# A trunk kernel on one core: pooling as doubled sums on DVE, eight buffers in the second norm, output weights scaled without GpSimd

## The chip, the cores and the metric

The kernel runs on one core of a Trainium2 chip. The metric is the device time of one execution in microseconds (us); a version is measured in several runs and judged by their median. The engines are called by their short names: PE multiplies matrices (PEld is its loading of weights), DVE is the vector engine, ACT the scalar engine, POOL is GpSimd, and SP issues transfers.

## The reference

What is computed is a decoder trunk of two layers over 1024 tokens of width 1024, in float32. Each layer has a mixer and a mixture of experts, both behind an RMS norm that is modulated by a conditioning vector:

```python
mod = (jax.nn.silu(c) @ w_mod[i] + b_mod[i])[:, None, :]
shift1, scale1, gate1, shift2, scale2, gate2 = jnp.split(mod, 6, axis=-1)
h = rmsnorm(x, norm_gain[i, 0]) * (1.0 + scale1) + shift1
y = pool_mixer(...) if i == 0 else gla_mixer(...)
x = x + gate1 * y
h = rmsnorm(x, norm_gain[i, 1]) * (1.0 + scale2) + shift2
x = x + gate2 * hier_moe(h, ...)
```

The pooling mixer takes, for four groups of 256 channels, the mean over the last 2, 4, 8 or 16 tokens (fewer at the start of the sequence) minus the token itself, multiplies it by a block-diagonal matrix, adds a bias and scales. The GLA mixer of the second layer is a chunked gated linear attention that ends in an output product with `gla_w_out`. The mixture of experts sends each token to two of 64 experts.

## The kernel before

The stages follow one another on one core, and each reads what the one ahead of it wrote.

**First norm and pooling.** `X[t]` (t = 0 to 7) holds 128 tokens by 1024 channels. `rows_load` (L169) brings one slice of the modulation weights `w_mod` into a ring of six slots, `rows_use` (L181) multiplies it on PE, and `mods(lo, hi)` uses slices `lo` to `hi - 1` and starts the load of the slice six further on; there are 24 slices, and six loads of GLA input weights (L831) follow them in the ring. Slices 0 to 7 give the first norm's shift, scale and gate. `xn_tile` (L240, L236, L237, L242) squares on ACT, takes the root, inverts on DVE and scales the tile into `xh[t % 3]`. `mix(t)` pools on PE: a product with a band matrix per group (L847, `band` or `first`), and a second one with the tail of the tile ahead (L850, `prev`); the result is the transposed, pooled tile `dT[t]` (L852). The band matrices are built on DVE (L811 to L818).

**The pooling's output.** Once slices 0 to 7 are in, `pw` is scaled by columns and rows (L218, L225, L869), `Q1` is the bias row (L865), GpSimd adds it to every tile (L884), and `mix_out(t)` multiplies `dT[t]` by `pw` on PE (L878) and adds the result to `X[t]` on DVE (L881). Between the tiles stand slices 8 to 15, two for each pair of tiles.

**Second norm.** Tile by tile: `xn_tile` into `xnb[t % 2]`, `route_turn` (a store to `h_d`, L260, and eight transposes, L250, drained by ACT at L257 and DVE at L255), one slice of the modulation (16 to 23), and the router's product (L268, L269). The two buffers `xnb` are read by the store to `h_d`. `route` then sorts the tokens, and the first layer's experts begin; their weights come on SP's queue (L514, L515).

**Between the layers.** During the experts, pieces ("units") of the GLA input product run on PE (L1041) from a list that `run_units(n)` works off. After the last expert the eighth tile is normed and turned (`prep_norm`, `prep_out`), `scale_wo` works out a scale for the output weights in three steps (L1107, L1114, L225 with L1122), and all engines meet a branch for lists of over 128 tokens (L1178), whose body isn't run with these inputs. The order on PE here is the order in which the code is written.

**GLA.** Behind the branch the rest of the units, the gates of tiles 0 and 1 (`gl_gate`, L1247 to L1275) and `split_wo` (L1128: each of eight output weight blocks times the scale, four on DVE and four on GpSimd; L1129 and L1130: split into two float16 parts) come ahead of the scores (L1283 to L1288), the mixing (L1312 to L1334), the turning (L1342) and the output product (L1353), tile by tile.

Of the kernel before, what the change touches and what calls it, by code (L numbers as in the profile page):

```python
# [11 lines left out]
AF = mybir.ActivationFunctionType  # L12
# [5 lines left out]
NT = 8  # L18
# [18 lines left out]
def trunk_kernel(ctx, tc, x_in, c_in, norm_gain, w_mod, b_mod, pool_w, pool_b, pool_scale,  # L37
# [765 lines left out]
    V.memset(XGt, 0.0)  # L803
    V.memset(part(15, 7, 1024), 0.0)
    m01 = part(15, 6, 128)
    rw = part(15, 6.5, 128)
    band = [part(1, 8 + g, 128) for g in range(4)]
    prev = [part(1, 8.5 + g, 128) for g in range(4)]
    first = [part(15, 8 + 0.5 * g, 128) for g in range(4)]
    for g, w in enumerate(WINDOWS):  # L810
        V.tensor_scalar(m01, dm, 0.0, None, op0=OP.is_ge)  # L811
        V.scalar_tensor_tensor(m01, dm, float(w), m01, op0=OP.is_lt, op1=OP.mult)
        V.scalar_tensor_tensor(band[g], m01, 1.0 / w, ident, op0=OP.mult, op1=OP.subtract)
        V.tensor_scalar(rw, slot_no, 1.0, float(w), op0=OP.add, op1=OP.min)
        V.reciprocal(rw, rw)
        V.tensor_tensor(m01, m01, rw, op=OP.mult)
        V.tensor_tensor(first[g], m01, ident, op=OP.subtract)
        V.tensor_scalar(prev[g], dm, float(w - 128), 1.0 / w, op0=OP.is_lt, op1=OP.mult)  # L818
# [15 lines left out]
    pcol = part(15, 10, 16)  # L834
    xh = [part(8, 4 * i, 1024) for i in range(3)]
# [24 lines left out]
    mod_scale(0, 0)  # L860
    V.tensor_tensor(pcol[:, 0:8], sec(0, 2), C2[:, 16:24], op=OP.mult)
    V.tensor_tensor(pcol[:, 8:16], pcol[:, 0:8], C2[:, 8:16], op=OP.mult)
    for half in range(2):
        s = slice(half * 512, half * 512 + 512)
        S.copy(Q1[:, s], row_psum(pcol[:, 8:16], half, dg[0]))  # L865
        p = row_psum(pcol[:, 0:8], half, dg[1])
        for j in range(4):
            kc = 4 * half + j
            V.scalar_tensor_tensor(pw[:, kc, :], pw[:, kc, :], modA[:, 0, 0, kc:kc + 1],  # L869
                                   p[:, j // 2 * 256:j // 2 * 256 + 256], op0=OP.mult, op1=OP.mult)  # L870
# [12 lines left out]
    for t in range(NT):  # L883
        G.tensor_tensor(X[t], X[t], Q1, op=OP.add)  # L884
    for t in range(4):
        mods(8 + 2 * t, 10 + 2 * t)
        mix_out(2 * t)
        mix_out(2 * t + 1)
    mod_scale(0, 1)
    gate2_rows(0, dg)  # L890
    for t in range(NT):
        xn_tile(t, xnb[t % 2], xnb[t % 2], 1)
        route_turn(t, 0, xnb[t % 2], hTb[t % 2])
        mods(16 + t, 17 + t)
        route_logits(t, hTb[t % 2], wr, L, brow)
# [117 lines left out]
    def prep_out(j):  # L1013
        turn_tile(1, 0, xs, lambda kc: xsv[:, kc, :], gmul, gadd)
        for k in (slice(0, 4), slice(4, 8)):
# [138 lines left out]
    with tc.manual_schedule(engines={ET.PE}):  # L1154
# [7 lines left out]
        prep_norm(7)  # L1162
        run_units(len(units))
# [199 lines left out]
    with tc.manual_schedule(engines={ET.PE}):  # L1363
# [7 lines left out]
        ins = gl_load_v(1)  # L1371
        gl_gate(1)
        with tc.issue_after(ins):
            split_wo()
# [158 lines left out]
```

## Time and profile before

| what | us |
|---|---|
| median of three runs | 2247.91 |
| the three runs | 2247.04, 2247.91, 2256.6 |
| the profiled execution | 2258.23 |
| its span, from the first to the last instruction | 2256.5 |
| PE busy in it | 1912.5 (85%) |
| DVE, ACT, POOL busy | 710.4, 621.8, 498.6 |
| moved by the transfers | 770.31 MB, 341 GB/s |

The profiled execution is one run with the profiler on; times inside it are counted from the start of its span. Busy shares are means over stages with different limits, so a part of the change is read from the rows of its own stage.

### The profile page before, as it was taken

What the parts mean: (1) busy time and instruction counts of PE and PEld (TensorE: products, weight loads), DVE (VectorE), ACT (ScalarE), POOL (GpSimd) and SP (SyncE); (2) the same over time, 40 slices, a digit from 0 to 9 for tenths busy, and PEclk for the clock granted to TensorE, in tenths of its full rate; (3) what the DMA queues carried; (4) which work ended last, traced back from release to release, by engine and by line L of the source; (5) the groups of instructions that cost most, each with busy time, mean ns of one, the idle gap of its engine ahead of it and who ended that gap; (6) DMA issues with size and microseconds to landing.
All of it is one profiled execution on the core that took longest, in us unless ns stands there. A gap on an engine that the chain in (4) does not pass through costs nothing. (4 is left out here: it accounts for less than half of the span.)

```text
span 2256.5 us, 31745 instructions
## 1 busy us (share of the span) xinstructions
PE 1912.5 (85%) x11311; PEld 924.9 (41%) x11312; DVE 710.4 (31%) x1762; ACT 621.8 (28%) x1425; POOL 498.6 (22%) x425
## 2 busy tenths in 40 slices
PE   7967889799999989898888999798977777788884
PEld 5644333344444444343344665433333333333331
DVE  3453544321121121212247677422211111122222
ACT  4232322332223131313136665212111111111122
POOL 0303221222222222222223110122222121212211
PEclk9988999999999999999998999999999999999997
DMA  9988987999998999999846843799999999999995
GB/s 351 368 316 332 395 335 292 390 355 357 387 347 325 365 365 372 368 357 384 340 127 207 326 132 120 303 403 399 406 386 408 383 390 404 397 398 399 399 398 169
DMA packets 173526, 770.31 MB, mean 341 GB/s; under 512 B 31711, under 2 KB 41357, under 8 KB 136382
## 3 DMA queue, kind: packets, MB, share of 16 engines
q1 hardware_dynamic: 127922, 684.66, 76.4%
q0 software_dynamic: 43952, 77.69, 12.3%
q10 hardware_dynamic: 1372, 4.28, 0.5%
q8 instruction: 170, 2.79, 0.5%
q14 instruction: 110, 0.90, 0.1%
HBM read 735.45 MB, written 69.80 MB: 357 GB/s over the span
## 5 line engine op out<-in xcount | busy, mean ns | idle before, releaser
L555 PE MATMUL ps<-slot,slot 128*64 128x384 f32 x2816 | 482.2, 491 | 63.7 <-DMA slot<-in_moe_w_in_dram 58.3
L580 PE MATMUL ps<-slot,slot 128*64 128x512 f32 x1656 | 405.8, 627 | 64.4 <-ACT slot L572 41.4
L555 PEld LDWEIGHTS ps<-slot,slot 128*64 128x64 f32 x2816 | 204.9, 138 | 350.3 <-issue 233.2
L586 POOL DMA_INDIRECT x_d<-kept x96 | 157.6, 1641 | 555.0 <-DVE kept L585 196.8
L1041 PE MATMUL ps<-slot,slot 128*128 128x512 f16 x1152 | 273.5, 383 | 7.3 <-DVEq L1178 5.8
L562 ACT ACTIVATE slot<-ps 64x384 f32<-64x384 f32 x88 | 42.7, 485 | 753.9 <-PE ps L555 718.1
L539 DVE TENSOR_SCALAR slot<-ps,kept 128x64 f32<-128x64 f32 x552 | 151.7, 335 | 262.0 <-PE ps L529 260.5
L580 PEld LDWEIGHTS ps<-slot,slot 128*64 128x64 f32 x1656 | 111.5, 141 | 264.1 <-issue 169.9
L563 DVE TENSOR_TENSOR slot<-slot,ps 64x384 f32<-64x384 f32 x88 | 48.6, 552 | 499.5 <-ACT slot L562 494.5
L537 ACT ACTIVATE slot<-ps,kept 128x64 f32<-128x64 f32 x552 | 178.5, 407 | 67.5 <-PE ps L529 34.4
L518 POOL DMA_INDIRECT kept<-h_d,kept x96 | 102.0, 1062 | 356.3 <-DMA x_d<-kept 146.8
L1041 PEld LDWEIGHTS <-slot 128*128 128x128 f16 x1152 | 112.4, 101 | 150.5 <-issue 44.6
L585 DVE SCALAR_TENSOR_TENSOR kept<-ps,kept 128x512 f32<-128x512 f32 x96 | 72.0, 750 | 257.5 <-PE ps L580 251.3
L1043 ACT ACTIVATE slot<-ps,slot 128x512 f32<-128x512 f32 x48 | 32.7, 686 | 415.3 <-PE ps L1041 409.4
L586 POOL DMA_INDIRECT x_d<-slot,kept x42 | 66.9, 1592 | 354.8 <-DVE slot L585 133.7
L618 PE MATMUL ps<-slot,slot 128*32 128x384 f32 x1216 | 107.2, 488 | 21.3 <-PEq L744 14.3
L571 PE MATMUL ps<-kept,slot 64*128 64x64 f32 x264 | 49.0, 293 | 56.0 <-DVE slot L563 53.0
L1353 PE MATMUL ps<-slot,slot 128*128 128x512 f16 x384 | 85.7, 379 | 1.2 <-DVE slot L1345 0.9
L618 PEld LDWEIGHTS ps<-slot,slot 128*32 128x32 f32 x1216 | 42.6, 109 | 79.0 <-issue 64.3
L622 PE MATMUL ps<-slot,slot 128*64 128x384 f32 x384 | 66.7, 501 | 9.0 <-PEq L744 5.5
L585 DVE SCALAR_TENSOR_TENSOR slot<-ps,kept 128x512 f32<-128x512 f32 x42 | 31.5, 751 | 124.5 <-PE ps L580 118.4
L529 PEld LDWEIGHTS ps<-kept 128*128 128x128 f32 x384 | 44.9, 164 | 60.3 <-issue 57.8
(359 smaller groups left out, 2027.9 us busy)
## 6 DMA issues: line engine op xcount, KB each, us to landing
slot<-in_moe_w_in_dram SPq DMA_DIRECT2D x256, 1536.0 KB
slot<-in_moe_w_out_dram SPq DMA_DIRECT2D x128, 1536.0 KB
slot<-in_w_mod_dram SPq DMA_DIRECT2D x24, 1536.0 KB
slot<-in_gla_w_in_dram SPq DMA_DIRECT2D x8, 1536.0 KB
slot<-in_w_mod_dram SPq DMA_DIRECT2D x8, 1152.0 KB
h_d<-slot POOLq DMA_DIRECT2D x16, 512.0 KB
slot<-in_x_dram SPq DMA_DIRECT2D x8, 512.0 KB
slot<-x_d POOLq DMA_DIRECT2D x8, 512.0 KB
```

What stands on the lines that cost most here:

```text
L518: return G.indirect_dma_start(out=XG[i], out_offset=None, in_=hv, in_offset=bass.IndirectOffsetOnAxis(ap=idx, axis=0), bounds_check=2 * SE ...
L537: S.activation(xT[:, cc, g, :], pv[:, g, :], AF.Identity, bias=sh, scale=sc)
L539: ins = V.tensor_scalar(xT[:, cc, g, :], pv[:, g, :], sc, sh, op0=OP.mult, op1=OP.add).ins
L555: T.matmul(p1[s, 0:384], xT[:, cc, g, :], W[:, u], start=n == 0, stop=n == 7)
L571: T.transpose(p3[:, cc * 64:(cc + 1) * 64], hh[:, :, cc], ident[s, s])
L580: T.matmul(p2[g * 64:g * 64 + 64, :], hT[:, cc * 64:(cc + 1) * 64], o[:, cc, g * 512:(g + 1) * 512], start=cc == 0, stop=cc == 2)
L585: V.scalar_tensor_tensor(XG[y], p2, w, G2, op0=OP.mult, op1=OP.mult)
L586: ins = G.indirect_dma_start(out=yv[l], out_offset=bass.IndirectOffsetOnAxis(ap=sidx, axis=0), in_=XG[y], in_offset=None, bounds_check=2 * ...
L618: T.matmul(p1[q:q + 32, 0:384], xT[:, cc, g, 0:32], weights(g, cc, u), start=n == 0, stop=n == 3)
L622: T.matmul(p1[64 * u:64 * u + 64, 0:384], xT[:, n % 4, n // 4, :], weights(n // 4, n % 4, u), start=n == 0, stop=n == 7)
L1041: T.matmul(p, hP[:, m, kc, :], W[:, n, :], start=kc + i == 0, stop=kc == KC - 1 and i == 2)
L1353: T.matmul(p, oT[:, m, kc, :], woh[kc][:, n, half * 512:(half + 1) * 512], start=kc + i == 0, stop=kc == KC - 1 and i == 2)
```

## The change

It has three parts. (1) `mix(t)` no longer multiplies by band matrices. PE turns the tile with one product per 128 channels against a diagonal of the norm's factors (L850 of the new file), ACT copies it into `hx[t % 2]` behind the last 16 columns of the tile ahead (L851, L845), and DVE builds the sums over 2, 4, 8 and 16 tokens by adding a sum to itself shifted (L855 to L858) and subtracts the token (L852, L867). The modulation slices are spread anew: 12 beside the pooling, four beside the output products. `Q1` is added on DVE behind each half tile (L898), and GpSimd clears `XGt` (L873), which DVE did. (2) The second norm has eight buffers. (3) `split_wo` runs on DVE alone, five of the eight blocks ahead of the branch and three behind it; `scale_wo` and the turning of the eighth tile come earlier, between units.

```diff
-    V.memset(XGt, 0.0)
...
     for g, w in enumerate(WINDOWS):
...
-        V.scalar_tensor_tensor(band[g], m01, 1.0 / w, ident, op0=OP.mult, op1=OP.subtract)
...
-        V.tensor_scalar(prev[g], dm, float(w - 128), 1.0 / w, op0=OP.is_lt, op1=OP.mult)
+        V.tensor_scalar(rw[g], slot_no[:, 0:16], 1.0, float(w), op0=OP.add, op1=OP.min)
+        V.reciprocal(rw[g], rw[g])
...
-    xnb = xh[0:2]
-    hTb = [xh[2], part(10, 8, 1024)]
+    hx = [part(8, 4.5 * i, 1152).rearrange("p (k n) -> p k n", k=KC) for i in range(2)]
+    flat_xg = XGt.rearrange("p a b -> p (a b)")
+    wa, wb = (flat_xg[:, 864 * i:864 * i + 864].rearrange("p (k n) -> p k n", k=6) for i in range(2))
+    xnb = [part(9, 4 * i, 1024) for i in range(3)] + [part(10, 4 * i, 1024) for i in range(2)] \
+        + [part(0, 4 * i, 1024) for i in range(3)]
+    hTb = [part(8, 4 * i, 1024) for i in range(2)]
...
     def mix(t):
-        h, d = xh[t % 3], dT[t]
+        h, d, dg = hx[t % 2], dT[t], rstd[t % 2]
+        st = stat[:, 0, t:t + 1]
+        S.activation(junk, X[t], AF.Square, accum_out=st)
+        rstd_of(st, st, D)
+        V.tensor_scalar(dg, ident, st, None, op0=OP.mult)
+        if t:
+            S.copy(h[:, :, 0:16], hx[(t - 1) % 2][:, :, 128:144])
         for b in range(2):
             p = ps()
             for j in range(4):
                 kc = 4 * b + j
-                g = kc // 2
-                T.matmul(p[:, j * 128:(j + 1) * 128], h[:, kc * 128:(kc + 1) * 128],
-                         band[g] if t else first[g], start=True, stop=t == 0)
-                if t:
-                    T.matmul(p[:, j * 128:(j + 1) * 128], xh[(t - 1) % 3][:, kc * 128:(kc + 1) * 128],
-                             prev[g], start=False, stop=True)
-            S.copy(d[:, 4 * b:4 * b + 4, :].rearrange("p k n -> p (k n)"), p)
+                T.matmul(p[:, j * 128:(j + 1) * 128], X[t][:, kc * 128:(kc + 1) * 128], dg, start=True, stop=True)
+            S.copy(h[:, 4 * b:4 * b + 4, 16:144], p.rearrange("p (k n) -> p k n", k=4))
+        V.tensor_tensor(d[:, 0:2, :], h[:, 0:2, 15:143], h[:, 0:2, 16:144], op=OP.subtract)
...
+        V.tensor_tensor(wa[:, :, 1:144], h[:, 2:8, 1:144], h[:, 2:8, 0:143], op=OP.add)
+        V.tensor_tensor(wb[:, :, 3:144], wa[:, :, 3:144], wa[:, :, 1:142], op=OP.add)
+        V.tensor_tensor(wa[:, 2:6, 7:144], wb[:, 2:6, 7:144], wb[:, 2:6, 3:140], op=OP.add)
+        V.tensor_tensor(wb[:, 4:6, 16:144], wa[:, 4:6, 16:144], wa[:, 4:6, 8:136], op=OP.add)
+        for g, w in list(enumerate(WINDOWS))[1:]:
...
+            V.scalar_tensor_tensor(d[:, ks, lo:128], m[:, :, 16 + lo:144], 1.0 / w, h[:, ks, 16 + lo:144],
+                                   op0=OP.mult, op1=OP.subtract)
 
     for t in range(NT):
-        xn_tile(t, xh[t % 3], xh[t % 3], 0)
-        if t < 6:
-            mods(t, t + 1)
         mix(t)
-    mods(6, 8)
+        mods(3 * t // 2, 3 * (t + 1) // 2)
+    G.memset(XGt, 0.0)
...
             V.tensor_tensor(xs, xs, p, op=OP.add)
-
-    for t in range(NT):
-        G.tensor_tensor(X[t], X[t], Q1, op=OP.add)
+            V.tensor_tensor(xs, xs, Q1[:, b * 512:(b + 1) * 512], op=OP.add)
+
     for t in range(4):
-        mods(8 + 2 * t, 10 + 2 * t)
+        mods(12 + t, 13 + t)
         mix_out(2 * t)
         mix_out(2 * t + 1)
...
-        xn_tile(t, xnb[t % 2], xnb[t % 2], 1)
-        route_turn(t, 0, xnb[t % 2], hTb[t % 2])
+        xn_tile(t, xnb[t], xnb[t], 1)
+        route_turn(t, 0, xnb[t], hTb[t % 2])
...
-    def split_wo():
-        for kc in range(KC):
+    def split_wo(lo, hi):
+        for kc in range(lo, hi):
             w, g = wo[kc], C2[:, 28 + kc % 2:29 + kc % 2]
-            (G if kc % 2 else V).tensor_tensor(w, w, XGt[:, 0:2, :].rearrange("p a b -> p (a b)"), op=OP.mult)
+            V.tensor_tensor(w, w, XGt[:, 0:2, :].rearrange("p a b -> p (a b)"), op=OP.mult)
...
         prep_norm(7)
+        run_units(22)
+        steps = scale_wo()
+        next(steps)
+        run_units(5)
+        next(steps)
+        with tc.high_priority():
+            prep_turn()
         run_units(len(units))
         with tc.high_priority():
-            prep_out(7)
-        run_units(9)
-        steps = scale_wo()
+            prep_out(7, False)
+        run_units(1)
         next(steps)
-        run_units(4)
-        next(steps)
-        run_units(4)
-        next(steps)
+        split_wo(0, 5)
+        run_units(16)
...
+        split_wo(5, KC)
...
-        with tc.issue_after(ins):
-            split_wo()
```

A group with a window of two tokens gets the plain difference of neighbours, so its factor of one half goes into the column scale of `pw`. Engines other than PE are ordered by a scheduler, so three places of the order are shown. In them `slot_66`, `slot_67`, `slot_74` to `slot_78`, `slot_80` and `slot_81` are the big buffers, `kept` holds small things and `XGt`, and `ps` is a bank of PE's output.

DVE beside the pooling, before: it builds the band matrices (L811 to L817) and scales tiles (L242).

```order
L242 TENSOR_SCALAR slot_74<-slot_78,kept 128x1024
L813 SCALAR_TENSOR_TENSOR slot_67<-slot_81,kept 128x128
L237 RECIPROCAL kept<-kept 128x1
L816 TENSOR_TENSOR slot_81<-slot_81 128x128
L242 TENSOR_SCALAR slot_74<-slot_78,kept 128x1024
L817 TENSOR_TENSOR slot_81<-slot_81,kept 128x128
```

DVE there now, one tile of eight: the sums (L855 to L858), the differences (L852, L867) and the diagonal of the tile after next (L843).

```order
L237 RECIPROCAL kept<-kept 128x1
L843 TENSOR_SCALAR slot_81<-kept 128x128
L855 TENSOR_TENSOR kept<-slot_74 128x6x143
L856 TENSOR_TENSOR kept<-kept 128x6x141
L852 TENSOR_TENSOR slot_75<-slot_74 128x256
L857 TENSOR_TENSOR kept<-kept 128x4x137
L867 SCALAR_TENSOR_TENSOR slot_66<-kept,slot_74 128x256
L858 TENSOR_TENSOR kept<-kept 128x2x128
L867 SCALAR_TENSOR_TENSOR slot_66<-kept,slot_74 128x256 x2
```

The pooling's arithmetic has moved from PE to DVE, which does it tile after tile in this order.

ACT in the second norm, before: the squares of a later tile (L240) stand between the drains of an earlier one (L257).

```order
L233 COPY kept<-ps 128x512
L257 ACTIVATE slot_74<-ps,kept 128x128 x2
L240 ACTIVATE slot_74,kept<-slot_78 128x1024
L257 ACTIVATE slot_74<-ps,kept 128x128 x2
L236 ACTIVATE kept<-kept 128x1
L257 ACTIVATE slot_76<-ps,kept 128x128 x3
L240 ACTIVATE slot_74,kept<-slot_79 128x1024
L257 ACTIVATE slot_76<-ps,kept 128x128
```

ACT there now.

```order
L240 ACTIVATE slot_66,kept<-slot_80 128x1024
L236 ACTIVATE kept<-kept 128x1
L240 ACTIVATE slot_76,kept<-slot_79 128x1024
L233 COPY kept<-ps 128x512
L257 ACTIVATE slot_74<-ps,kept 128x128 x2
L236 ACTIVATE kept<-kept 128x1
L240 ACTIVATE slot_66,kept<-slot_80 128x1024
L257 ACTIVATE slot_74<-ps,kept 128x128 x3
L236 ACTIVATE kept<-kept 128x1
L257 ACTIVATE slot_74<-ps,kept 128x128 x26
```

Seven of the eight squares now stand ahead of the drains or beside the first of them.

DVE around the branch, before: the last step ahead of it (L161, L1178), and what comes behind it.

```order
L218 TENSOR_TENSOR slot_76<-kept 128x512 x2
L161 TENSOR_REDUCE kept<-ps 128x3
L1178 TENSOR_LOAD kept
```

```order
L1183 COPY slot_77<-kept 128x256
L1213 MEMSET kept 128x512
L1216 TENSOR_TENSOR slot_77<-kept 128x128
L1214 MEMSET kept 128x8
L1217 MEMSET slot_77 32x128
L1128 TENSOR_TENSOR slot_66<-slot_66,kept 128x1024 x2
L1128 TENSOR_TENSOR slot_67<-slot_67,kept 128x1024
L1130 SCALAR_TENSOR_TENSOR slot_76<-slot_66,kept,slot_76 128x1024
```

DVE there now, ahead of the branch (L1201) and behind it.

```order
L1147 TENSOR_TENSOR slot_66<-slot_66,kept 128x1024 x3
L1149 SCALAR_TENSOR_TENSOR slot_76<-slot_66,kept,slot_76 128x1024 x2
L1147 TENSOR_TENSOR slot_67<-slot_67,kept 128x1024
L1149 SCALAR_TENSOR_TENSOR slot_66<-slot_66,kept 128x1024
L1147 TENSOR_TENSOR slot_67<-slot_67,kept 128x1024
L1149 SCALAR_TENSOR_TENSOR slot_66<-slot_67,kept,slot_66 128x1024 x2
L161 TENSOR_REDUCE kept<-ps 128x3
L163 TENSOR_TENSOR kept<-kept 128x3
L1201 TENSOR_LOAD kept
```

```order
L1207 COPY slot_77<-kept 128x256
L1147 TENSOR_TENSOR slot_67<-slot_67,kept 128x1024
L1147 TENSOR_TENSOR slot_77<-slot_77,kept 128x1024 x2
L1149 SCALAR_TENSOR_TENSOR slot_67<-slot_67,kept 128x1024
L1149 SCALAR_TENSOR_TENSOR slot_67<-slot_77,kept,slot_67 128x1024
L1238 MEMSET kept 128x512
```

Five blocks of the output weights have moved ahead of the branch, and none is left on GpSimd.

## Rows read from the trace of the kernel before

**Rows 1.** Stretches: length, busy time of PE, PEld, DVE, ACT, POOL; PE clock, transfer share, GB/s.

```profile
64.40:102.90 38.50, 38.40 (x238) 27.57 (x234) 17.68 (x28) 3.84 (x8) 16.70 (x9) 1.00 0.96 392
102.90:151.40 48.50, 39.49 (x328) 27.24 (x327) 19.69 (x58) 22.49 (x53) 3.20 (x6) 0.89 0.83 302
172.90:1117.60 944.70, 827.98 (x4849) 371.75 (x4845) 249.16 (x591) 246.91 (x581) 228.10 (x199) 0.97 0.96 359
```

**Rows 2.** Timeline, PE, pooling and its output: start, length, what, count [idle ahead <- releaser].

```profile
20.06 0.83 PE L847 MATMUL ps<-slot,slot 128*128 128x128 f32 x6
...
50.30 2.77 PE L181 MATMUL ps<-slot,slot 128*32 128x384 f32 x24
...
64.38 7.17 PE L878 MATMUL ps<-slot,slot 128*128 128x256 f32 x32
71.48 2.79 PE L181 MATMUL ps<-slot,slot 128*32 128x384 f32 x32
```

**Rows 3.** Timeline of ACT and SP in the first stage.

```profile
12.27 0.29 ACT L236 ACTIVATE kept<-kept 128x1 f32<-128x1 f32 x1
...
37.63 72.32 SPq L169 DMA_DIRECT2D slot<-in_w_mod_dram  x18
```

**Rows 4.** Timeline, DVE: lengths of adds and fused operations, elsewhere in the kernel.

```profile
1205.50 0.42 DVE L1270 TENSOR_TENSOR slot<-slot,slot 128x256 f32<-128x256 f32 x1
1205.83 0.42 DVE L1272 TENSOR_TENSOR slot<-ps,slot 128x256 f32<-128x256 f32 x1
...
1169.80 3.49 DVE L1128 TENSOR_TENSOR slot<-slot,kept 128x1024 f32<-128x1024 f32 x3
1173.20 1.28 DVE L1130 SCALAR_TENSOR_TENSOR slot<-slot,kept,slot 128x1024 f16<-128x1024 f32 x1
...
58.23 1.66 DVE L869 SCALAR_TENSOR_TENSOR slot<-slot,kept,ps 128x256 f32<-128x256 f32 x4 [0.17 <-PE ps L225]
59.80 0.68 DVE L218 TENSOR_TENSOR slot<-kept,slot 128x512 f32<-128x512 f32 x1
```

**Rows 5.** Groups by line, POOL: a clearing of 1024 elements (busy, mean ns).

```profile
L1478 POOL MEMSET kept<- 128x1024 f32 x1 | 1.0, 951 | 7.5 <-DVE kept L269 7.5
```

**Rows 6.** Timeline, PE, second norm: its modulation slices, one ahead of each tile's product.

```profile
103.93 1.50 PE L181 MATMUL ps<-slot,slot 128*32 128x384 f32 x16
...
108.07 1.50 PE L181 MATMUL ps<-slot,slot 128*32 128x384 f32 x16
...
122.30 2.79 PE L181 MATMUL ps<-slot,slot 128*32 128x384 f32 x16
...
146.76 1.50 PE L181 MATMUL ps<-slot,slot 128*32 128x384 f32 x16
```

**Rows 7.** Waits from 102.9 to 151.4: who waited <- for whom, us in total, times, longest.

```profile
ACT slot L240 <- DMA h_d<-slot: 10.3, 3, 5.2
...
PE ps L268 <- ACT slot L257: 8.5, 2, 4.6
```

**Rows 8.** Timeline, PE, around the branch.

```profile
1160.05 0.55 PE L159 MATMUL ps<-kept,slot 128*128 128x128 f32 x3 [0.60 <-ACT slot L154]
1166.39 8.16 PE L1041 MATMUL ps<-slot,slot 128*128 128x512 f16 x27 [5.79 <-DVEq L1178]
```

**Rows 9.** Timelines of DVE, POOL and PE, from the gates of GLA to its first turning.

```profile
1189.06 9.67 DVE L1270 TENSOR_TENSOR slot<-slot,slot 128x256 f32<-128x256 f32 x1
...
1189.17 9.27 POOL L1128 TENSOR_TENSOR slot<-slot,kept 128x1024 f32<-128x1024 f32 x4
...
1199.54 0.66 PE L1283 MATMUL ps<-slot 128*128 128x64 f32 x2 [3.81 <-DVE slot L1273]
...
1208.80 3.45 PE L1312 MATMUL ps<-slot,slot 128*128 128x256 f32 x8 [3.38 <-DVE slot L1288]
...
1213.82 0.33 PE L1283 MATMUL ps<-slot 128*128 128x64 f32 x2
...
1217.11 0.70 PE L1312 MATMUL ps<-slot,slot 128*128 128x256 f32 x2
```

More of the change, by code (lines that the diff above doesn't have):

```diff
@@ L801, in trunk_kernel @@
     SP.dma_start(wz, gla_w_in[0][:, 3072:3088].rearrange("(k p) f -> p k f", p=128))
-    V.memset(XGt, 0.0)
     V.memset(part(15, 7, 1024), 0.0)
[L805 to L809, printed above, removed]
-    for g, w in enumerate(WINDOWS):
-        V.tensor_scalar(m01, dm, 0.0, None, op0=OP.is_ge)
-        V.scalar_tensor_tensor(m01, dm, float(w), m01, op0=OP.is_lt, op1=OP.mult)
-        V.scalar_tensor_tensor(band[g], m01, 1.0 / w, ident, op0=OP.mult, op1=OP.subtract)
[L814 to L817, printed above, removed]
-        V.tensor_scalar(prev[g], dm, float(w - 128), 1.0 / w, op0=OP.is_lt, op1=OP.mult)
+    rw = [part(15, 6 + 0.0625 * g, 16) for g in range(4)]
+    for g, w in enumerate(WINDOWS):
+        V.tensor_scalar(rw[g], slot_no[:, 0:16], 1.0, float(w), op0=OP.add, op1=OP.min)
+        V.reciprocal(rw[g], rw[g])
     todo = [(l, half, kc) for l, half in ((0, 0), (0, 1), (1, 0)) for kc in range(KC)]
@@ L833, in trunk_kernel @@
     Q1 = part(14, 8, 1024)
-    pcol = part(15, 10, 16)
-    xh = [part(8, 4 * i, 1024) for i in range(3)]
+    pcol = part(15, 10, 24)
+    junk = part(10, 8, 1024)
+    rstd = [part(15, 8 + 0.5 * i, 128) for i in range(2)]
     dT = [part((0, 9, 10)[t // 3], 4 * (t % 3), 1024).rearrange("p (k n) -> p k n", k=KC) for t in range(NT)]
-    xnb = xh[0:2]
-    hTb = [xh[2], part(10, 8, 1024)]
-    def mix(t):
-        h, d = xh[t % 3], dT[t]
+    hx = [part(8, 4.5 * i, 1152).rearrange("p (k n) -> p k n", k=KC) for i in range(2)]
[4 more added lines that the diff above has]
+    hTb = [part(8, 4 * i, 1024) for i in range(2)]
+    G.memset(hx[0][:, :, 0:16], 0.0)
+    def mix(t):
+        h, d, dg = hx[t % 2], dT[t], rstd[t % 2]
[5 more added lines that the diff above has]
+            S.copy(h[:, :, 0:16], hx[(t - 1) % 2][:, :, 128:144])
         for b in range(2):
@@ L845, in mix @@
                 kc = 4 * b + j
-                g = kc // 2
-                T.matmul(p[:, j * 128:(j + 1) * 128], h[:, kc * 128:(kc + 1) * 128],
-                         band[g] if t else first[g], start=True, stop=t == 0)
-                if t:
-                    T.matmul(p[:, j * 128:(j + 1) * 128], xh[(t - 1) % 3][:, kc * 128:(kc + 1) * 128],
-                             prev[g], start=False, stop=True)
-            S.copy(d[:, 4 * b:4 * b + 4, :].rearrange("p k n -> p (k n)"), p)
+                T.matmul(p[:, j * 128:(j + 1) * 128], X[t][:, kc * 128:(kc + 1) * 128], dg, start=True, stop=True)
+            S.copy(h[:, 4 * b:4 * b + 4, 16:144], p.rearrange("p (k n) -> p k n", k=4))
+        V.tensor_tensor(d[:, 0:2, :], h[:, 0:2, 15:143], h[:, 0:2, 16:144], op=OP.subtract)
+        if t == 0:
+            G.memset(d[:, 0:2, 0:1], 0.0)
+        V.tensor_tensor(wa[:, :, 1:144], h[:, 2:8, 1:144], h[:, 2:8, 0:143], op=OP.add)
[3 more added lines that the diff above has]
+        for g, w in list(enumerate(WINDOWS))[1:]:
+            ks = slice(2 * g, 2 * g + 2)
+            m = (wb if g % 2 else wa)[:, 2 * g - 2:2 * g]
+            lo = 0
+            if t == 0:
+                lo = 16
+                V.tensor_tensor(m[:, :, 16:32], m[:, :, 16:32], rw[g][:, None, :].to_broadcast([128, 2, 16]), op=OP.mult)
+                V.tensor_tensor(d[:, ks, 0:16], m[:, :, 16:32], h[:, ks, 16:32], op=OP.subtract)
+            V.scalar_tensor_tensor(d[:, ks, lo:128], m[:, :, 16 + lo:144], 1.0 / w, h[:, ks, 16 + lo:144],
+                                   op0=OP.mult, op1=OP.subtract)
     for t in range(NT):
-        xn_tile(t, xh[t % 3], xh[t % 3], 0)
-        if t < 6:
-            mods(t, t + 1)
         mix(t)
-    mods(6, 8)
+        mods(3 * t // 2, 3 * (t + 1) // 2)
+    G.memset(XGt, 0.0)
     mod_scale(0, 0)
+    V.tensor_copy(pcol[:, 16:24], modA[:, 0, 0, :])
+    V.tensor_scalar(pcol[:, 16:18], pcol[:, 16:18], 0.5, None, op0=OP.mult)
     V.tensor_tensor(pcol[:, 0:8], sec(0, 2), C2[:, 16:24], op=OP.mult)
@@ L868, in trunk_kernel @@
             kc = 4 * half + j
-            V.scalar_tensor_tensor(pw[:, kc, :], pw[:, kc, :], modA[:, 0, 0, kc:kc + 1],
+            V.scalar_tensor_tensor(pw[:, kc, :], pw[:, kc, :], pcol[:, 16 + kc:17 + kc],
                                    p[:, j // 2 * 256:j // 2 * 256 + 256], op0=OP.mult, op1=OP.mult)
@@ L1011, in prep_norm, with prep_turn, prep_out @@
         V.tensor_scalar(xs, xs, st, None, op0=OP.mult)
-    def prep_out(j):
+    def prep_turn():
         turn_tile(1, 0, xs, lambda kc: xsv[:, kc, :], gmul, gadd)
+    def prep_out(j, turn=True):
+        if turn:
+            prep_turn()
         for k in (slice(0, 4), slice(4, 8)):
@@ L1181, in trunk_kernel @@
             load_wo()
+            split_wo(0, 5)
         units += kept_units
@@ L1370, in trunk_kernel @@
         gl_load_v(0)
-        ins = gl_load_v(1)
+        gl_load_v(1)
         gl_gate(1)
-        with tc.issue_after(ins):
-            split_wo()
         for a in AT:
```

1 line of the change is left out of this document (added).

## The prediction

> **What bounds the kernel now.** I read the stretches first, then the timelines of the three places that the change touches. The stretches [rows 1] show that the two mixtures of experts hold most of the time: in the first one, from 172.9 to 1117.6, the transfers are busy 96% of the time and PE 88%. The change leaves them alone. Their loads follow the routing, so a stage ahead of them that ends earlier moves them as a whole, and the sum is that of three stages.
>
> In the pooling PE is the bound. A product of 128 by 128 advances it by 0.22 us (six entries, three products, in 0.67 us), the tiles follow without idle time until slices 6 and 7 are used at 50.30, and only then can the scale of `pw` be worked out, so that the first output product starts at 64.38 [rows 2]. From there to 102.9 PE is busy all the time [rows 1]. The second norm is different: PE is busy 39.5 of 48.5 us at a mean clock of 0.89 [rows 1]. The modulation slices mark its tiles: 103.93, 108.07, then 122.30 for the fourth [rows 6]. In the waits the reader sees why: ACT's squares wait for the store to `h_d` to release one of two buffers, 10.3 us in all, the drains stand behind them on ACT's queue, and PE waits 8.5 us for the drains [rows 7]. In GLA a multiplication on DVE that takes 0.42 us elsewhere [rows 4] takes 9.67, exactly beside the four multiplications of `split_wo` on POOL, 9.27 us [rows 9].
>
> **The change, part by part.** Removed from PE in the pooling: 56 products with `prev` of 0.22 us [rows 2], and from DVE the band matrices. PE isn't what ends this stage any more, so these are costed at nothing; DVE is. Its work for a tile is four adds and a difference over 858, 846, 548, 256 and 256 elements, three fused operations over 256, an inversion and a diagonal. An add of 1024 takes 1.16 us (3.49 for three) and one of 256 takes 0.42 [rows 4], so an element costs about 0.96 ns: 1.00, 0.99, 0.70, 0.42 and 0.42, in sum 3.5. The fused ones cost 0.42 each by the four of L869 (1.66) [rows 4], 1.3 together, and the small ones 0.4. Operations that don't need each other overlap by 0.08 (two start 0.33 apart and take 0.42 [rows 4]), five times a tile. That makes 4.9 us a tile, 39 for eight, and 1 more for the first tile's short window.
>
> The chain starts when the first root ends at 12.56 [rows 3]; inversion, diagonal, eight products, 1.8, and ACT's copies take me to about 17. Into DVE's order fall four spreads (L218) of 0.68 and eight scalings of `pw` of 0.4 [rows 4], 6 us, and about 2 us of waits: SP starts the loads of slices 6 and following at 37.63 [rows 3] whatever PE does, so at about 4 us a slice (1.5 MB at 392 GB/s [rows 1]) slice 8 lands near 49, and tile 6 stands behind it on PE. So 17 + 40 + 6 + 2 = 65, and PE's first output product comes at about 65.4, **1.0 later**. Bounds: 4.4 a tile if more of it overlaps, 3 us earlier; 5.6 if nothing does, 6.6 later.
>
> GpSimd's clearing of `XGt` costs 1.9 us (two of 951 ns [rows 5]) just when the last spreads run. Since POOL's multiplications held a DVE operation up for their whole length [rows 9], it could hold these up by 0 to 1.9; the row nearest to it reads as POOL does there and a clearing reads nothing, so I take 0. The Trainium skill (SBUF — State Buffer, Who interferes with whom) says that a DVE instruction with two SBUF inputs contends with a GpSimd instruction that reads SBUF, not with one that only writes; by that rule it is 0 as well, by a rule that any GpSimd work locks DVE out it would be 1.9, and no row here decides between them.
>
> In the output products four slices remain for eight. Three pairs of 2.79 [rows 2] stand between them before; four single ones of 1.4 now: **2.8 less**. The added `Q1` halves on DVE, 16 of 0.68, with 16 drains of 0.69 and the scaling of eight tiles, stay under PE's 36 us there. If DVE fell behind, tiles 6 and 7 would be late. PE's clock is the unknown: PE now waits for DVE through the pooling and may start the products at 1.2 GHz. After the stop in the second norm a slice took 2.79 in place of 1.50 [rows 6]; a few microseconds at that level give 0 to 4, and I take **2 more**.
>
> In the second norm eight buffers take the store out of the way, and seven squares are done before the drains. Eight tiles at the undisturbed step of 4.15 (103.93 to 108.07) need 29.1 from the first slice to the last; it was 42.8 (103.93 to 146.76) [rows 6]: **13 less**, at worst the 8.5 of PE's wait alone [rows 7]. Its DMAs: eight stores and the six GLA loads now fall into 36 us, with two slices some 14 MB, about 36 us at 392 GB/s [rows 1]; the first expert's loads queue behind them, but are asked for only after the routing.
>
> Ahead of the branch, PE keeps the same units, and the turning of the last tile no longer stops it. DVE's ten operations of `split_wo`, five of 1.16 and five of 1.28 [rows 4], 12.2 us, start when `XGt` is filled and lie beside 16 units; both end near 1158 by my count, where PE reached the branch at 1160.6 [rows 8]: **2 less**, between 3 less and 2 more. The 5.79 of the branch itself stay [rows 8].
>
> Behind it DVE has three blocks, 7.3 us, in place of four multiplications and eight fused ones. POOL's four go, and with them PE's idle 3.81 and 3.38; the scores then also run at full clock, 3.3 (1213.82 to 1217.11) in place of 5.9 (1199.54 to 1205.42), and the eight products of L1312 in half of 3.45 [rows 9]. That is 3.8 + 3.4 + 2.6 + 1.7: **11 less** (the waits alone, 7, are the lower bound; 13 if the gates come early as well). Next late there would be the rows of `r`, fetched only after the last unit has been written out.
>
> Sum: 1.0 - 2.8 + 2 - 13 - 2 - 11 = -25.8. The profiled execution took 2258.23; that makes 2232.4. The median of the runs is 2247.91, 10.3 below it, and I carry the difference over: 2222.1.
>
> **The rivals.** *The pooling turns into the bound, and half as fast* (slower). If the shifted adds cost twice as much per element, a tile takes 4.8 more, eight take 38, and the sum is +12.6: 2260.5. It decides from 8.1 us a tile on, where the whole gain of 25.8 is used up. Against it: the 0.42 of L1270 and L1272 [rows 4] are operations over 64-element runs already, at the common rate. For it: no row has both inputs out of one buffer, shifted.
>
> *PE at the low clock* from the pooling into the second norm: the output products, 28.7 us at full clock by four groups of 7.17 [rows 2], would need twice that in the worst case; with half of it the first stage's gain of 12.8 is gone, and the time is about 2235. For it: the mean clock was 0.89 in the second norm and PE was busy 81% of it [rows 1]. Against it: PE still runs 12 slices and 64 products among the sums. The Trainium skill (TensorE: Matmul & The Clock Gate, What's actually happening) says that the throttled clock is the default and activity releases it; by that rule this rival is live, and the trace agrees in that slices after a stop ran at half rate.
>
> *A new wait in GLA or at the branch*: if `r` or DVE's three blocks come late by 8, 13 less become 5, and the time is 2230. *The experts' loads don't start earlier*, since stores and GLA loads hold the queue: 2235 too; I count it with the clock.
>
> **How the numbers follow.** My forecast has 0.68, the clock or the queue 0.16, the new wait 0.10, the slow adds 0.06. About 0.5%, 11.2 us, is what a measurement of this kernel can tell from no change: the lines are 2236.7 and 2259.2. The forecast is faster; of the second case half is, of the third 0.06; of the last 0.04 is slower. So faster 0.82, same 0.14, slower 0.04. The range goes from 2211, most bounds at their good end, to 2241, most at their bad end with the clock lost.
>
> **What would show it.** In the profile after: DVE without a break from about 17 to 65 at 4.9 us a tile; the first output product near 65; second-norm slices 4.2 apart and no wait of L240 for `h_d`; the experts' first loads 13 us earlier; no POOL multiplication, no DVE entry of 9 us, and the scores of tile 0 right behind the last unit. A tile of 6 us or more on DVE, a PE clock well under 1.00 in the output products, or a PE stop behind the branch would make it wrong.

## The result and the profile after

| what | before | changed |
|---|---|---|
| median of the first runs, four each, us | 2250.24 | 2226.66 |
| profiled execution | 2258.23 | 2224.01 |
| its span | 2256.5 | 2222.3 |

The medians differ by 23.6 us, where 25.8 were forecast. The ratio of the runs is 0.9887, with an interval of 0.986 to 0.9914, that is 19 to 32 us. Two later measurements on other chips gave 0.9904 [0.9879, 0.993] and 0.9891 [0.9866, 0.9916]. The profiled pair differs by 34.2 us, more than the medians: the first profile of before lies 8 us above its median, and what that execution lost is told below.

The stretches, with the same columns as [rows 1]; the second norm now ends at about 139, and its window holds part of the routing:

```profile
64.40:102.90 38.50, 38.30 (x213) 27.11 (x205) 28.66 (x52) 9.55 (x21) 4.12 (x6) 0.97 0.99 401
102.90:151.40 48.50, 39.06 (x357) 26.91 (x356) 31.66 (x111) 19.79 (x45) 2.06 (x4) 0.90 0.89 347
```

PE at the end of the pooling, to be held against [rows 2]. The slice at 63.21 waits for its transfer, and the second scale of `pw` (L225) follows it; the first output product comes at 68.11 in place of 64.38:

```profile
52.35 3.62 PE L850 MATMUL ps<-slot,slot 128*128 128x128 f32 x30
...
57.65 1.88 PE L225 MATMUL ps<-slot,kept 128*128 128x512 f32 x4
59.53 1.50 PE L181 MATMUL ps<-slot,slot 128*32 128x384 f32 x16
63.21 2.64 PE L181 MATMUL ps<-slot,slot 128*32 128x384 f32 x16 [2.18 <-DMA slot<-in_w_mod_dram]
65.78 2.49 PE L225 MATMUL ps<-slot,kept 128*128 128x512 f32 x4
68.11 1.89 PE L894 MATMUL ps<-slot,slot 128*128 128x256 f32 x8
...
78.16 7.17 PE L894 MATMUL ps<-slot,slot 128*128 128x256 f32 x32
```

DVE, the sums of one tile and then the end of the pooling. The adds take 1.05, 1.04 and 0.72. The two spreads (L218) for the second half of `pw` stand behind the last tile's sums:

```profile
28.95 1.05 DVE L855 TENSOR_TENSOR kept<-slot 128x858 f32<-128x858 f32 x1
30.03 1.04 DVE L856 TENSOR_TENSOR kept<-kept 128x846 f32<-128x846 f32 x1
30.99 0.42 DVE L852 TENSOR_TENSOR slot<-slot 128x256 f32<-128x256 f32 x1
31.32 0.72 DVE L857 TENSOR_TENSOR kept<-kept 128x548 f32<-128x548 f32 x1
...
52.60 0.68 DVE L218 TENSOR_TENSOR slot<-kept,slot 128x512 f32<-128x512 f32 x1
...
63.43 0.76 DVE L867 SCALAR_TENSOR_TENSOR slot<-kept,slot 128x256 f32<-128x256 f32 x2
64.10 0.87 DVE L885 SCALAR_TENSOR_TENSOR slot<-slot,slot,ps 128x256 f32<-128x256 f32 x2
64.88 1.29 DVE L218 TENSOR_TENSOR slot<-kept,slot 128x512 f32<-128x512 f32 x2
68.31 1.66 DVE L885 SCALAR_TENSOR_TENSOR slot<-slot,slot,ps 128x256 f32<-128x256 f32 x4 [2.14 <-PE ps L225]
```

POOL clears `XGt` beside those two spreads, which take no longer for it (1.29 for two, 0.68 for one):

```profile
64.24 1.81 POOL L873 MEMSET kept<- 128x2048 f32 x1 [47.36 <-DVE slot L867]
```

The slices of the second norm on PE, against [rows 6]. All eight are 4.14 to 4.24 apart:

```profile
105.46 1.50 PE L181 MATMUL ps<-slot,slot 128*32 128x384 f32 x16
109.60 1.50 PE L181 MATMUL ps<-slot,slot 128*32 128x384 f32 x16
...
134.97 1.50 PE L181 MATMUL ps<-slot,slot 128*32 128x384 f32 x16
```

And in the waits of this stretch, against [rows 7], ACT's squares no longer wait for `h_d`:

```profile
ACT slot L240 <- PE ps L894: 0.4, 1, 0.4
```

PE around the branch, against [rows 8]. It is reached 25.7 us earlier, and its idle time has grown from 5.79 to 7.06:

```profile
1134.40 0.55 PE L159 MATMUL ps<-kept,slot 128*128 128x128 f32 x3 [0.60 <-ACT slot L154]
1142.01 7.67 PE L1060 MATMUL ps<-slot,slot 128*128 128x512 f16 x27 [7.06 <-DVEq L1201]
```

GLA, one row of DVE and then PE, against [rows 9]. The gate's multiplication takes 0.42 and not 9.67, the scores follow the last unit without a wait and at the full clock, and the slice ahead of the first output product now waits 1.17 us for its transfer:

```profile
1163.09 0.42 DVE L1295 TENSOR_TENSOR slot<-slot,slot 128x256 f32<-128x256 f32 x1
...
1170.38 0.49 PE L159 MATMUL ps<-kept,slot 128*128 128x128 f32 x3
1170.71 0.33 PE L1308 MATMUL ps<-slot 128*128 128x64 f32 x2
...
1174.00 1.99 PE L1337 MATMUL ps<-slot,slot 128*128 128x256 f32 x8
...
1190.69 1.50 PE L152 MATMUL ps<-slot,slot 128*32 128x384 f32 x16 [1.17 <-DMA slot<-in_w_mod_dram]
1192.12 5.35 PE L1378 MATMUL ps<-slot,slot 128*128 128x512 f16 x24
```

### The profile page after: what moved, and what is told of

Read it like the earlier page. It is cut to its first block, busy times and chain, and to the rows that moved or that the text cites. A ratio compares the mean times of both kernels' runs of the same rounds, so it can differ in the third digit from the quotient of the medians.

```text
span 2222.3 us, 31618 instructions
## 1 busy us (share of the span) xinstructions
PE 1891.1 (85%) x11199; PEld 908.6 (41%) x11200; DVE 735.3 (33%) x1829; ACT 624.3 (28%) x1432; POOL 469.4 (21%) x416
## 5 line engine op out<-in xcount | busy, mean ns | idle before, releaser
L618 PE MATMUL ps<-slot,slot 128*32 128x384 f32 x1216 | 108.0, 491 | 21.6 <-PEq L744 14.3
L622 PE MATMUL ps<-slot,slot 128*64 128x384 f32 x384 | 64.6, 488 | 6.4 <-PEq L744 5.4
## 6 DMA issues: line engine op xcount, KB each, us to landing
slot<-in_moe_w_out_dram SPq DMA_DIRECT2D x128, 1536.0 KB, 12.7
```

The costliest lines, as they stand in the source:

```text
L618: T.matmul(p1[q:q + 32, 0:384], xT[:, cc, g, 0:32], weights(g, cc, u), start=n == 0, stop=n == 3)
L622: T.matmul(p1[64 * u:64 * u + 64, 0:384], xT[:, n % 4, n // 4, :], weights(n // 4, n % 4, u), start=n == 0, stop=n == 7)
```

## The experiments

Each kernel ran beside before on the same chip; the ratio is to that. The first four are before once more and each part of the change alone.

**Before again.** Nothing changed.

> The kernel before once more, nothing changed. The two profiled executions differ by 34.2 us (spans 2256.5 and 2222.3), the medians by 23.6. Theory: some 10 us of the profiled one of before belong to that execution alone, in the stretch between the first router table on PE (L421) and the first expert's first product (L622), which took 23.7 us there and 13.5 in the changed kernel, with idle time put down to 'issue' and 'remote'. Then a second profile has about 14 us in that stretch and a span near 2246. Rival: the stretch is long in every execution of before, because its expert loads meet the tables later in the queue; then it takes about 24 us again, and the 10 us are lost elsewhere in other executions.

Measured: 2252.46, span 2250.7. From the first table to the first expert it took 23.5 us, about as in the first profile (23.7). (The tables are the products of L421 with which `route` sorts the tokens; the first expert starts with L622.) The rival holds. PE at this place, then DVE: the table products come in small groups with idle time in which PE waits for nothing that the profile shows ("issue"), and DVE stands still for 13.42 until something that the profile can't name ("remote"):

```profile
161.09 10.68 PE L421 MATMUL ps<-slot,slot 128*64 128x64 f32 x170 [2.44 <-DVE slot L488]
171.92 0.65 PE L421 MATMUL ps<-slot,slot 128*64 128x192 f32 x5 [0.15 <-issue]
173.38 0.56 PE L421 MATMUL ps<-slot,slot 128*64 128x192 f32 x4 [0.81 <-issue]
...
184.55 2.19 PE L622 MATMUL ps<-slot,slot 128*64 128x384 f32 x6 [2.85 <-remote]
```

```profile
169.95 0.21 DVE L442 COPY kept<-ps 128x64 f32<-128x64 f32 x1
183.59 0.28 DVE L431 TENSOR_SCALAR kept<-ps,kept 128x64 int32<-128x64 f32 x1 [13.42 <-remote]
```

What differed instead was the second norm: from its first slice to its last 37.26 us here, 42.83 in the first profile. The waits for the store are not the same from one execution to the next.

**The pooling alone:** the diff's first part, with two buffers `xnb` and `split_wo` as before.

> Part 1 of the change alone: pooling by doubled sums, the modulation slices spread anew, Q1 on DVE; two buffers in the second norm and the output weights as before. Theory (shares add, as the milestones in the two traces say): the first output product 3.7 us later, the first slice of the second norm 1.5 later, so 2252 against 2250, ratio 1.000 to 1.002. Rival A: the pooling itself is a gain by my prediction's other end (2 to 3 us earlier), ratio 0.999. Rival B: DVE's sums alone, without the buffers behind them, push the second norm into new waits: 5 us or more slower, ratio 1.002 or more.

Measured: 2257.47 against 2256.83, ratio 1.0005 [0.9982, 1.0029]. First output product at 67.77. No gain and no loss that can be told; rival B's 1.002 or more is not excluded, as the interval reaches 1.0029.

**The buffers alone** (part 2).

```diff
-    xnb = xh[0:2]
-    hTb = [xh[2], part(10, 8, 1024)]
+    xnb = [part(9, 4 * i, 1024) for i in range(3)] + [part(10, 4 * i, 1024) for i in range(2)] \
+        + [part(0, 4 * i, 1024) for i in range(3)]
+    hTb = [part(8, 4 * i, 1024) for i in range(2)]
```

> Part 2 alone: eight buffers in the second norm of the kernel before. Theory: the last slice of the second norm comes 13 us earlier, the first expert's loads with it, and the time falls by 12 to 13: ratio 0.9945. Rival: the loads behind the norm (stores and GLA weights) hold the queue, so that half or more is given back ahead of the first expert: 3 to 7 us, ratio 0.997 to 0.999.

Measured: ratio 0.9963 [0.9945, 0.9981], 8.3 us of 2256.83, between the two forecasts. The slices take 29.51 from first to last. The first expert loads are asked for 7.3 us earlier than in before's second profile (144.45 for 151.74), 12.7 earlier than in its first, and the first expert starts 7.4 earlier (177.16 for 184.55). So the rival's reason isn't seen: nothing is given back ahead of the first expert. The theory's size was off, because the execution that I read had lost more in this stage than the other.

**The output weights alone:** the diff from `prep_turn` on, and nothing ahead of it.

> Part 3 alone: output weights scaled on DVE, five of eight blocks ahead of the branch, the scale and the turning of the eighth tile earlier. Theory: the branch is reached 3 us earlier and GLA loses its two PE waits and a stretch at half clock, less 1.3 at the branch and some waits for modulation slices: 12 us, ratio 0.9947. Rival: part of that needs the earlier arrival that the other parts bring (transfers in flight at the branch), and alone it is worth 5 to 8: ratio 0.9965 to 0.998.

Measured: ratio 0.9929 [0.9908, 0.995], 16 us. From the end of the branch to the first output product of GLA it took 52.07 us, where before took 62.37 and 62.84. The theory holds in kind, and the gain doesn't need the other parts; the 12 us that it forecast lie inside the interval (11 to 21).

**The changed kernel again.**

> The changed kernel once more, nothing else changed, beside before on one chip. In its first profile the stretch from the first router table on PE to the first expert took 13.5 us; in before, its repeat and each part alone it took 23.5 to 24.7, with the same instructions in the same order on PE, DVE and ACT. Theory A (the parts add): part 2 gains 8 us alone and part 3 gains 16, the pooling 0, so 24 in sum, ratio 0.989; the missing stall was one execution's luck and the stretch takes about 24 us in a second profile. Theory B: the stall is gone for good in the changed kernel, since its tables meet the expert loads at another moment; then the stretch takes about 13.5 again, and the ratio is 0.985 or less.

Measured: 2227.4 against 2250.73, ratio 0.9904 [0.9879, 0.993]. The tables ran through without a stop, 13.5 us in all, PE and then DVE:

```profile
155.37 12.45 PE L421 MATMUL ps<-slot,slot 128*64 128x64 f32 x192 [2.35 <-DVE slot L488]
167.76 0.66 PE L529 MATMUL ps<-kept 128*128 128x128 f32 x4
```

```profile
167.86 0.28 DVE L431 TENSOR_SCALAR kept<-ps,kept 128x64 int32<-128x64 f32 x1 [4.78 <-PE ps L421]
```

The missing stall was no luck, as theory B has it, but the ratio is nearer to theory A's. How both can be is told in the next section.

**Parts 1 and 2 together:** the diff up to the second norm, and nothing from `prep_turn` on.

> Parts 1 and 2 together, the output weights as before. Theory A (parts add): 8 us faster than before, ratio 0.9965, and a stretch of 24 us from the first table to the first expert. Theory B (the two together do away with that stall of 10 us): 18 us faster, ratio 0.992, and a stretch of 13.5.

Measured: 2238.96, ratio 0.9948 [0.9927, 0.997], 11.7 us; the stretch took 13.6. The stretch is theory B's. The ratio lies between the two, with theory A's 0.9965 inside the interval and theory B's 0.992 just outside.

**All on DVE at the old place.** Before, with GpSimd's share of `split_wo` given to DVE and nothing moved:

```diff
-            (G if kc % 2 else V).tensor_tensor(w, w, XGt[:, 0:2, :].rearrange("p a b -> p (a b)"), op=OP.mult)
+            V.tensor_tensor(w, w, XGt[:, 0:2, :].rearrange("p a b -> p (a b)"), op=OP.mult)
```

> Before with one word changed: all eight multiplications of the output weights run on DVE, at their old place behind the branch; nothing is moved. Theory (GpSimd is what held DVE up): the 9.67 us of the gate's multiplication fall to 0.42 and four multiplications of 1.16 come in their place on DVE, ahead of the gates: PE's two waits of 3.8 and 3.4 shrink, 4 to 8 us faster, ratio 0.9965 to 0.998. Rival (it is DVE's load behind the branch, not GpSimd): DVE has 4.6 us more ahead of the gates, so the scores come as late as before or later: ratio 0.999 to 1.002.

Measured: 2251.22 against 2250.73, ratio 0.9995 [0.9974, 1.0016]. The ratio is the rival's, the profile the theory's: the gate's multiplication is short, and the branch's end to GLA's first output product takes 55.73, 6.9 less than before's mean of 62.6. But a wait of 4.14 is left on PE, ahead of the mixing:

```profile
1187.78 0.42 DVE L1270 TENSOR_TENSOR slot<-slot,slot 128x256 f32<-128x256 f32 x1
...
1189.78 1.23 DVE L1128 TENSOR_TENSOR slot<-slot,kept 128x1024 f32<-128x1024 f32 x1
```

```profile
1199.10 3.75 PE L1312 MATMUL ps<-slot,slot 128*128 128x256 f32 x8 [4.14 <-issue]
```

That the whole time did not fall is not explained by this: the interval allows up to 5.9 us of gain.

**GpSimd at the new place.** The changed kernel, odd blocks on GpSimd again:

```diff
-            V.tensor_tensor(w, w, XGt[:, 0:2, :].rearrange("p a b -> p (a b)"), op=OP.mult)
+            (G if kc % 2 else V).tensor_tensor(w, w, XGt[:, 0:2, :].rearrange("p a b -> p (a b)"), op=OP.mult)
```

> The changed kernel with the four odd blocks of the output weights multiplied on GpSimd again, at their new places (two ahead of the branch, two behind it). Theory (GpSimd's multiplication holds a DVE operation with two inputs up for its whole length of some 9 us): ahead of the branch it costs up to 5 us at the arrival at the branch, behind it DVE's next blocks or the gates are held up; 3 to 10 us slower than the changed kernel, ratio to before 0.990 to 0.994. Rival (only the move counts): as the changed kernel, 0.987 to 0.989.

Measured: 2236.01, 8.6 us over the changed kernel beside it, ratio 0.9929 [0.9908, 0.995]. The theory holds in kind. POOL, then DVE:

```profile
1129.07 6.68 POOL L1147 TENSOR_TENSOR slot<-slot,kept 128x1024 f32<-128x1024 f32 x2 [1.41 <-ACT kept L1141]
1152.62 4.69 POOL L1147 TENSOR_TENSOR slot<-slot,kept 128x1024 f32<-128x1024 f32 x2 [16.87 <-SPq L1201]
```

```profile
1129.02 4.51 DVE L1147 TENSOR_TENSOR slot<-slot,kept 128x1024 f32<-128x1024 f32 x2 [1.60 <-ACT kept L1141]
1133.66 4.36 DVE L1149 SCALAR_TENSOR_TENSOR slot<-slot,kept,slot 128x1024 f16<-128x1024 f32 x2
...
1152.62 2.48 DVE L1207 COPY slot<-kept 128x256 f32<-128x256 f32 x1 [0.73 <-SPq L1201]
1155.03 3.36 DVE L1147 TENSOR_TENSOR slot<-slot,kept 128x1024 f32<-128x1024 f32 x1
```

The two multiplications take 4.51 for 2.36, the two fused operations 4.36 for 2.47, the copy 2.48 for 0.29. For the copy, the changed kernel's first profile has:

```profile
1143.12 0.29 DVE L1207 COPY slot<-kept 128x256 f32<-128x256 f32 x1 [0.89 <-SPq L1201]
```

From the last expert to the end of the branch it took 51.2 us, where the changed kernel needs 46.4 to 49.8, 47.7 in the mean: GpSimd costs about 3 there. Behind the branch the gates come late enough not to meet it: 51.9 to the first output product, as in the changed kernel. The rest of the 8.6 isn't explained: of the 11.3 us between the two profiles, taken side by side, 6.3 lie behind that product, where GpSimd's work is the same.

**The changed kernel a third time,** as the measure for the next two.

> The changed kernel a third time, as the measure for the two variants beside it: ratio to before 0.988 to 0.991, first output product of the pooling at 68, last slice of the second norm at 135 to 136, stretch from the first router table to the first expert 13.5 us (24 if the missing stall were luck).

Measured: 2228.56 against 2254.42, ratio 0.9891 [0.9866, 0.9916]; first output product 67.56, last slice 134.42, stretch 13.55.

**Without the pooling:** the buffers as in the diff above, and the diff from `prep_turn` on.

> The changed kernel with its part 1 undone: pooling with band matrices on PE, the slices as before, Q1 on GpSimd; eight buffers and the output weights as changed. Theory (the pooling is worth nothing, its first output product 3.7 us later, its second norm's start 1.5 to 2.3 later): 1 to 3 us faster than the changed kernel, ratio to before 0.987 to 0.990, last slice near 133.5. Rival (parts 1 and 2 gain together what neither gains alone: 11.7 us against 8 and 0): 3 us or more slower than the changed kernel.

Measured: 2227.65, 0.9 under the changed kernel beside it, ratio 0.9897 [0.9874, 0.9921]; last slice at 133.96. The rival's 3 us don't show. With the pooling alone at 1.0005, the new pooling brings nothing that can be measured.

**Own buffers for the second half's spreads.** The changed kernel with

```diff
-        S.copy(Q1[:, s], row_psum(pcol[:, 8:16], half, dg[0]))
-        p = row_psum(pcol[:, 0:8], half, dg[1])
+        dh = [part(10, 8 + 2 * i, 512) for i in range(2)] if half else dg
+        S.copy(Q1[:, s], row_psum(pcol[:, 8:16], half, dh[0]))
+        p = row_psum(pcol[:, 0:8], half, dh[1])
```

> The changed kernel with two more small buffers, so that the two spreads of pw's scale for the second half need not wait until PE has read those of the first half: DVE then makes all four ahead of the last tiles' sums. Theory (the first output product is late because those spreads stand behind the last tile's sums on DVE and the last four scalings behind them): it comes 3 us earlier, at 65, the second norm's first slice 1 to 3 earlier, and the time falls by 1 to 3 us. Rival (slice 12, which PE waits for ahead of it, sets the moment): the first output product starts earlier but the stage ends as before, within 0.5 us.

Measured: 2223.63, 4.9 us under the changed kernel beside it, ratio to before 0.988 [0.9854, 0.9905]. DVE has the four spreads behind each other, PE multiplies all eight at once, and the first output product comes at 63.22:

```profile
52.46 0.68 DVE L218 TENSOR_TENSOR slot<-kept,slot 128x512 f32<-128x512 f32 x1
53.13 1.89 DVE L218 TENSOR_TENSOR slot<-kept,slot 128x512 f32<-128x512 f32 x3
```

```profile
58.26 3.60 PE L225 MATMUL ps<-slot,kept 128*128 128x512 f32 x8
61.79 1.50 PE L181 MATMUL ps<-slot,slot 128*32 128x384 f32 x16
63.22 1.13 PE L895 MATMUL ps<-slot,slot 128*128 128x256 f32 x4
...
66.30 1.50 PE L181 MATMUL ps<-slot,slot 128*32 128x384 f32 x16
```

PE's order here is the scheduler's too, and it has changed with the edit: the slice that stands ahead of the first output product in the changed kernel (at 63.21 in its first profile, where it waits for its transfer) now stands behind it, at 66.30. So the earlier start isn't the spreads' alone. The second norm's first slice comes at 103.44, 1.5 earlier than in the one profile of the kernel beside it; the rest of the 4.9 is within the spread of the runs. This kernel has the lowest median of all kernels here, but the intervals of its ratio and the changed kernel's overlap.

**All on DVE at the old place, again.**

> The kernel with all eight multiplications on DVE at their old place, once more, for the stretch between the first router table and the first expert. It took 13.8 us in its first profile, 23.7 and 23.5 in the two of before, whose instructions on PE, DVE and ACT up to there are the same. Theory (it goes with the program): 13.8 again. Rival (each execution has its luck): 24 in this one is as likely as not.

Measured: 2244.72; the stretch took 14.3. The theory holds: it goes with the program.

## Why the prediction was right, and where it was off

The moments on PE, from the two profiles of before and the three of the changed kernel (means of each, differences in us):

| stretch | forecast | before | changed | difference |
|---|---|---|---|---|
| to the second norm's first slice | +0.2 | 103.93, 104.07 | 105.46, 106.22, 104.90 | +1.5 |
| to its last slice | -13 | 42.83, 37.26 | 29.51, 29.51, 29.52 | -10.5 |
| to the units behind the last expert | 0 | 970.83, 966.49 | 960.27, 960.71, 966.80 | -6.1 |
| to the end of the branch | -2 | 48.80, 51.29 | 46.77, 49.82, 46.37 | -2.4 |
| to GLA's first output product | -11 | 62.37, 62.84 | 50.11, 52.32, 50.48 | -11.6 |
| to the end | 0 | 1027.74, 1028.75 | 1030.18, 1026.52, 1030.13 | +0.7 |

The sum is -28.4 over these five executions; the three medians say -23.6, -23.3 and -25.9. Single runs of before on one chip went from 2247 to 2269, so five profiles fix their sum to a few microseconds only.

That the total came out within 4.6 us (2222.1 forecast, 2226.66 measured) is in part luck. The second norm gave 2.5 less than forecast and the first output product came 2.7 later, while the experts, put at 0, gave 6. And the 10.3 us by which before's profiled execution lay above its median were carried over to the forecast, but the changed kernel's profiled execution (2224.01) lies 2.7 under its median.

**First output product, +1.0.** Measured +3.7. DVE does the sums at the lengths forecast (858 elements in 1.05 for 1.00, the fused ones 0.42), 4.4 to 5.1 us a tile where nothing is waited for. Two terms failed. The first is "four spreads of 0.68 and eight scalings of 0.4, 6 us" as work that merely adds up. Two spreads share their buffers with the first two, so they wait until PE has read those; by then DVE is in the last tile's sums, and PE waits for the spreads, as the changed kernel's second profile shows:

```profile
63.91 1.50 PE L181 MATMUL ps<-slot,slot 128*32 128x384 f32 x16 [1.59 <-DMA slot<-in_w_mod_dram]
67.08 1.96 PE L225 MATMUL ps<-slot,kept 128*128 128x512 f32 x4 [1.67 <-DVE slot L218]
```

The kernel with own buffers takes that wait away and starts at 63.22, with the slice behind. The second term is "about 2 us of waits": between the first sum at 17.34 and the end of the last spread at 66.17 DVE stood still for 6.6 us, longest for a copy of ACT's:

```profile
41.02 0.42 DVE L852 TENSOR_TENSOR slot<-slot 128x256 f32<-128x256 f32 x1 [2.68 <-ACT slot L851]
```

The upper bound, 5.6 a tile "if nothing does" overlap, doesn't follow from the prediction's own lengths: they add up to 5.2 without any overlap, 3.4 later and not 6.6.

**Four fewer slices, -2.8,** and **clock, +2.** From the first output product to the next stage it took 39.55 before and 37.35 now: 2.2 less, and the products ran at 2.4 GHz: 32 of them take 7.17 at 78.16, as in [rows 2]. Ahead of them the clock did fall. PE had waited 2.18 us for the slice at 63.21, and the granted clock was 0.61 from 63 to 65 us and 0.54 from 65 to 67. That slice took 2.64 and the L225 behind it 2.49, where the second profile, at the full clock, has 1.50 and 1.96. These 1.7 us at the 1.2 GHz level belong to the first output product, and only a part of them lies on the path, since without them PE waits 1.67 for the spreads. By the Trainium skill (TensorE: Matmul & The Clock Gate, What's actually happening) the throttled clock is the default and activity releases it; the trace agrees in that the slice behind the wait ran at about half rate.

**Second norm, -13.** Right in kind, and 29.5 was measured where 29.1 was forecast. What failed is the time that 29.1 was taken from: 42.83 was one execution's, 37.26 another's, which makes 10.5 in the mean. The four other profiles with two buffers have 35.82, 36.41, 42.87 and 35.69; over all six the gain is 9.0, close to the 8.3 of the buffers alone. (42.8 less 29.1 is 13.7, too, and not 13.)

**Experts, 0.** Here the prediction missed something. In before, its repeat and each part alone, 23.5 to 24.7 us passed between the first table and the first expert; in the changed kernel, the two pairs of parts that were tried, all on DVE at the old place and the two other variants, 13.2 to 14.3. About six of those ten microseconds are still there when the last expert is done. The medians don't show it as clearly: all on DVE at the old place has lost the stall too, and is not faster than before by more than 5.9.

**Branch, -2.** Measured -2.4, though the branch itself takes longer: 6.6 to 7.7 us of PE's idle time wherever part 3 is in, 5.4 to 5.9 where it isn't. That is 1.4 in the means of seven profiles each. Its cause stays open: the body that the branch skips holds `split_wo(0, 5)` with part 3, up to ten more instructions on DVE, but no run leaves that out alone.

**GLA, -11.** Measured -11.6. The two halves of part 3 don't add up here: with all on DVE at the old place the stretch is 6.7 shorter than before (55.73 and 56.19), with GpSimd at the new place 10.7 (51.88).

**The rivals.** Slow adds: no. The experts' loads held by the queue: no, they are asked for 10.4 us after the last slice in before and 10.9 after it now. A new wait in GLA: yes, but small: PE waits 4.8, 1.2 and 5.0 us in the three profiles for modulation slices between 1185 and 1445, where before waited for none; it is inside the differences above. GpSimd's clearing at no cost: right, the two spreads at 64.88 took 1.29 beside it. By the Trainium skill (SBUF — State Buffer, Who interferes with whom) a DVE instruction with two inputs in SBUF doesn't contend with a GpSimd instruction that only writes; the two spreads agree.

## What to carry to other kernels

A wait's price read from one execution is one sample: the stage of the two buffers lost 13.3 us in one profile and 7.7 in the next, so profile the kernel before twice when a gain rests on a wait for a transfer. Moving work off a contended engine pays where the waiting engine then has room. On one chip, the swap to DVE alone gave nothing that the time shows (2251.22 for 2250.73), the move with GpSimd kept gave 2.9 over parts 1 and 2 (2236.01 for 2238.96), and both together 11.6 (2227.4). Before counting work on an in-order engine as a sum, look which of it shares a buffer with something that another engine still reads.

## What the runs showed of the hardware that was not expected

The stall ahead of the first expert belongs to the program, not to the execution or the schedule. Four programs have it (before in two profiles), six don't (the changed one in three, all on DVE at the old place in two), with the same order of instructions on PE, DVE and ACT at that place, with two buffers or eight. During it PE's products come in small groups with gaps of 0.15 to 0.88 us, and DVE and ACT go on together, 2.0 us after the end of GpSimd's last gather in each of the five profiles; in the programs without it they don't wait for the gathers. All on DVE at the old place differs from before only in and after `split_wo`, a thousand microseconds later, has PE's instructions in the very same order from first to last, and lacks it. The transfers of instructions that the traces show come at nearly the same moments in these two (169.92, 174.66 and 179.32 in before, 169.92, 174.32 and 179.52 there), so they don't tell them apart. What property of the program decides was not found, and stays open.

In the one profile that has it, a one-input copy on DVE beside GpSimd's multiplication took 2.48 for 0.29. The Trainium skill (SBUF — State Buffer, Who interferes with whom) says that copies can enter a mode that takes the shared port; the row agrees.
